# A row softmax on one core: sixteen partitions of the third tile loaded first, and no row of the second tile split

## The chip, the cores and the metric

The kernel runs on one core of one Trainium2 chip. The metric is the device time of a run in microseconds. The profile is one execution taken by the hardware profiler; its span runs from the first to the last instruction and is shorter than the time of a run by what lies around the program.

## The reference

```python
batch, seq, dim = 16, 1024, 512          # x: float32
x_scaled = x / 2.0
x_max = np.max(x_scaled, axis=-1, keepdims=True)
exp_x = np.exp(x_scaled - x_max)
return exp_x / np.sum(exp_x, axis=-1, keepdims=True)
```

There are 16384 rows of 512 numbers, 33.55 MB in and 33.55 MB out.

## The kernel before

Each of the 128 partitions works on 128 rows. They are cut into ten tiles along `TILES`, pairs of (rows per partition, place in the arena): 3, 5, and then eight times 15 rows. A tile is contiguous in memory, and partition p holds its rows p·r to p·r + r - 1, so a partition of a tile is one run of r·2048 bytes: 6 KB in tile 0, 10 KB in tile 1, 30 KB in the tiles from 2 on ("the third tile"). The arena in SBUF holds 98 rows per partition. Tiles 0 to 7 fill it; tiles 8 and 9 (`LATE`) reuse the places of tiles 0 to 3 and are loaded by GpSimd once those tiles' stores have landed.

The fast path leaves the maximum out. ACT takes the exponential of half of each row in place, with the row's sum as an accumulated output (`stats`); DVE takes the reciprocal of the sums and multiplies a group of rows in place; SyncE stores a tile when its multiplications are done. At the end a count of the sums that lie in a safe range is made through TensorE, and a slow path with the maximum (`rounds`) runs if a sum lies outside; in the profile it does not run.

What sets the order around the change:

- `early()` is put ahead of the start barrier of the program. There SyncE issues the load of tile 0, and ACT issues the load of tile 1.
- `loads()` comes behind the barrier: ACT issues the loads of tiles 2 to 7, one after another. Then ACT loads its table (line 200) and begins the exponentials.
- SyncE's DMAs go to one queue (q1 in the profile, which also carries all the stores), ACT's to another (q10), GpSimd's to a third (q0). All three share 16 DMA engines.
- TensorE waits for the tiles in order (line 194): a tile's semaphore `ld[t]` counts 16 for each DMA. For each tile it raises `s_go` by the number of chunks that begin there, and ACT takes these tokens one by one (`take`, line 140). A chunk is 3 rows for tile 0 and 5 rows after it.
- DVE waits for the exponentials of one to three chunks (line 166), multiplies (line 169), and SyncE stores (line 137).

The load of tile 1 is made of three DMAs: four rows of every partition, the last row of partitions 0 to 125, and the last row of partitions 126 and 127 (`SPREAD`, lines 113 to 121). So this tile's semaphore counts to 48.

Of the kernel before, what the change touches and what calls it, by code (L numbers as in the profile page):

```python
# [16 lines left out]
HEAD = [3]  # L17
E = 5

SPREAD = 1  # L20

TURN = 83

# [5 lines left out]
def kernel(  # L29
# [5 lines left out]
    nc = tc.nc  # L35
# [6 lines left out]
    xf = x.flatten_outer_dims()  # L42
    of = out.flatten_outer_dims()
    N, D = xf.shape
    P = nc.NUM_PARTITIONS
# [14 lines left out]
    tiles, base = [], 0  # L60
# [5 lines left out]
    def dram(ap, t):  # L66
        b, r, _ = tiles[t]
        return ap[b * P : (b + r) * P].rearrange("(p r) d -> p r d", r=r)

    def sb(t):  # L70
        _, r, at = tiles[t]
        return arena[:, at : at + r, :]
# [5 lines left out]
    owner = [max(t for t, (b, _, _) in enumerate(tiles) if b <= s) for s in starts]  # L78
# [12 lines left out]
    ld = [nc.alloc_semaphore(f"ld{t}") for t in range(len(tiles))]  # L91
# [4 lines left out]
    s_go = nc.alloc_semaphore("s_go")  # L96
# [13 lines left out]
    g_rec = nc.alloc_semaphore("g_rec")  # L110
    g_mul = nc.alloc_semaphore("g_mul")

    def load(eng, t):
        r = tiles[t][1]
        parts = [(0, P, 0, r)]
        if t == SPREAD:
            parts = [(0, P, 0, r - 1), (0, 126, r - 1, r), (126, P, r - 1, r)]
        for p, q, lo, hi in parts:
            eng.dma_start(  # L119
                out=sb(t)[p:q, lo:hi], in_=dram(xf, t)[p:q, lo:hi]  # L120
            ).then_inc(ld[t], 16)

    stored_by = {u: s_home[t] for t, us in LATE.items() for u in us}
    for t, (_, r, at) in enumerate(tiles):
# [26 lines left out]
            eng.reg_add(i, i, 1)  # L151

    def early():
        load(nc.sync, 0)
        load(nc.scalar, 1)

    def loads():
        for t in range(2, min(LATE)):
            load(nc.scalar, t)

    def program():

        for j, ks in enumerate(pairs):
# [3 lines left out]
                out=recip[:, b : b + c], in_=stats[:, b : b + c]  # L167
            )._wait_ge(s_exp, ks[-1] + 1).then_inc(s_rec, 1)
            nc.vector.tensor_mul(  # L169
                out=arena[:, a : a + c],  # L170
# [6 lines left out]
        for t, us in LATE.items():  # L177
# [3 lines left out]
            out=inside[:, :], in0=stats[:, :], scalar1=LO, scalar2=HI,  # L181
# [3 lines left out]
            out=inside[:, :], in0=inside[:, :], scalar=1.0, in1=stats[:, :],  # L185
# [3 lines left out]
            out=flag[:, :], in0=total[:, :], scalar1=float(N), scalar2=None, op0=Alu.is_ge,  # L189
# [1 line left out]


        for t in range(len(tiles)):
            nc.tensor.wait_ge(ld[t], 48 if t == SPREAD else 16).then_inc(s_go, owner.count(t))
        nc.tensor.wait_ge(s_ones, 1)
        nc.tensor.matmul(  # L196
            total[:, :], lhsT=count[:, :], rhs=ones[:, :], start=True, stop=True
# [3 lines left out]
        for k, c in enumerate(HEAD):  # L201
            take(nc.scalar, s_go, 1)
            for b in range(starts[k], starts[k] + c):
                ins = nc.scalar.activation(  # L204
                    out=arena[:, b], in_=arena[:, b], func=Exp, scale=0.5,
# [75 lines left out]
    entry.instructions = []  # L281
    nc.switch_bb("main", None)
    early()
    first = list(entry.instructions)
    at = next(k for k, i in enumerate(head) if type(i).__name__ == "InstDrain")
    entry.instructions = head[:at] + first + head[at:]
    act = []
    entry.instructions = list(entry.instructions) + [i for i in jumps if i not in act]
    nc.switch_body(here, parent=None, valid_engines=[i.engine for i in jumps])
    loads()  # L290
    program()


# [28 lines left out]
```

## Time and profile before

| | |
|---|---|
| time of a run, median of 3 | 159.94 us (159.79 to 166.79) |
| span of the profiled execution | 158.7 us |
| bytes moved | 67.11 MB, on average 423 GB/s over the span |
| packets | 3024, of these 336 under 512 B (the semaphore packets) and 720 under 8 KB |
| ACT busy | 80.8 us (51%) |
| DVE busy | 73.2 us (46%) |
| load of tile 0, issue to landing | 5.6 us |

The profiled execution has no time of its own beside its span; the median of the runs is 1.2 us above it. All numbers are microseconds unless marked otherwise. L119 is line 119 of the kernel; an engine name with a q behind it (SPq, ACTq) is the engine's instruction queue. The trace also holds a record of every DMA packet: its queue, start, duration and bytes, but not the number of its engine.

### The profile page before, as it was taken

The page shows a single profiled execution, that of the slowest core. Times are in us where ns is not written, and L with a number is a line of the kernel's source. Part 1 is how long each engine was busy: PE and PEld are TensorE (multiplying, and loading weights), DVE is VectorE, ACT ScalarE, POOL GpSimd, SP SyncE. Part 2 cuts the span into 40 slices and gives each one's busy share as a digit, 9 for nine tenths or more (in the row PEclk, how much of TensorE's full clock was granted, in tenths as well). Part 3 has the DMA queues.
Part 4 walks back from the last instruction along what each step waited for, and adds up shares of the span by engine and source line. Part 5 has one row for each costly group of instructions (what it writes and reads, how often), then busy time and mean ns, then how long its engine had stood idle before and what let it go on. Part 6 is the DMA issues. An engine that isn't in the chain of part 4 may idle for free. (4 is left out here: it accounts for less than half of the span.)

```text
span 158.7 us, 657 instructions
## 1 busy us (share of the span) xinstructions
PE 0.2 (0%) x2; PEld 0.1 (0%) x2; DVE 73.2 (46%) x27; ACT 80.8 (51%) x257; POOL 2.2 (1%) x8
## 2 busy tenths in 40 slices
PE   0000000000000000000000000000000000000000
PEld 0000000000000000000000000000000000000000
DVE  0047001992981990059500991008932981992000
ACT  0590598697498008940399001991597009940000
POOL 0000000000000000000000300000000000010000
DMA  7999998989999999999999999999999999999995
GB/s 271 382 496 396 463 437 324 480 382 485 410 457 410 457 410 449 418 449 418 441 426 441 426 434 434 426 441 426 441 418 449 418 449 410 457 403 465 403 457 256
DMA packets 3024, 67.11 MB, mean 423 GB/s; under 512 B 336, under 2 KB 336, under 8 KB 720
## 3 DMA queue, kind: packets, MB, share of 16 engines
q1 hardware_dynamic: 1584, 34.34, 50.4%
q10 hardware_dynamic: 1152, 24.90, 37.1%
q0 software_dynamic: 288, 7.86, 11.5%
HBM read 33.55 MB, written 33.55 MB: 423 GB/s over the span
## 5 line engine op out<-in xcount | busy, mean ns | idle before, releaser
L271 ACT ACTIVATE arena<-arena x125 | 76.8, 615 | 54.1 <-ACTq L140 54.1
L169 DVE TENSOR_TENSOR arena<-arena,recip 128x7680 f32<-128x7680 f32 (+2 forms) x12 | 70.2, 5847 | 0.4
L166 DVE RECIPROCAL recip<-stats 128x15 f32<-128x15 f32 (+2 forms) x12 | 2.7, 224 | 70.4 <-ACT arena L271 61.4
L271 ACT ACTIVATION_READ_ACCUMULATOR arena<-arena x125 | 23.4, 187 | 0.0
L200 ACT ACT_TABLE_LOAD x1 | 1.3, 1283 | 5.7 <-issue 5.7
L119 POOL DMA_DIRECT2D arena<-in_x_dram x2 | 1.3, 638 | 84.9 <-ACT arena L271 84.9
L204 ACT ACTIVATE arena<-arena 128x512 f32<-128x512 f32 x3 | 1.9, 619 | 0.0
L180 POOL TENSOR_SCALAR inside<-stats 128x128 f32<-128x128 f32 x1 | 0.6, 630 | 51.7 <-ACT arena L271 51.7
L204 ACT ACTIVATION_READ_ACCUMULATOR arena<-arena 128x1 f32 x3 | 0.6, 188 | 0.0
L196 PE MATMUL total<-ones,count 128*1 128x1 f32 x2 | 0.2, 164 | 143.9 <-DVE inside L184 143.9
L184 DVE SCALAR_TENSOR_TENSOR inside<-inside,stats 128x128 f32<-128x128 f32 x1 | 0.3, 282 | 0.0
L188 DVE TENSOR_SCALAR flag<-total 1x1 int32<-1x1 f32 x1 | 0.1, 146 | 0.3 <-PE total L196 0.3
L196 PEld LDWEIGHTS total<-ones,count 128*1 128x1 f32 x2 | 0.1, 80 | 143.9 <-DVE inside L184 143.9
L175 POOL MEMSET ones<- 128x1 f32 x1 | 0.1, 98 | 2.2 <-POOLq L37 2.2
L306 POOL MEMSET const-bfloat16-1.0<- 128x1 bf16 x1 | 0.1, 108 | 0.0
L306 POOL MEMSET const-uint8-127<- 128x1 uint8 x1 | 0.1, 108 | 0.0
L306 POOL MEMSET const-float32-0.0<- 128x1 f32 x1 | 0.1, 104 | 0.2 <-issue 0.2
L306 POOL MEMSET const-float32-1.0<- 128x1 f32 x1 | 0.1, 104 | 0.0
L184 DVE DVE_READ_ACCUMULATOR inside<-inside,stats 128x1 f32 x1 | 0.1, 80 | 0.0
## 6 DMA issues: line engine op xcount, KB each, us to landing
out_dram<-arena SPq DMA_DIRECT2D x8, 3840.0 KB, 26.2
arena<-in_x_dram ACTq DMA_DIRECT2D x6, 3840.0 KB, 46.7
arena<-in_x_dram POOLq DMA_DIRECT2D x2, 3840.0 KB, 33.6
out_dram<-arena SPq DMA_DIRECT2D x1, 1280.0 KB, 22.9
arena<-in_x_dram ACTq DMA_DIRECT2D x1, 1024.0 KB
arena<-in_x_dram SPq DMA_DIRECT2D x1, 768.0 KB, 5.6
out_dram<-arena SPq DMA_DIRECT2D x1, 768.0 KB, 14.6
arena<-in_x_dram ACTq DMA_DIRECT2D x1, 252.0 KB
```

Of the source, the lines that this page charges most:

```text
L119: eng.dma_start(out=sb(t)[p:q, lo:hi], in_=dram(xf, t)[p:q, lo:hi]).then_inc(ld[t], 16)
L166: nc.vector.reciprocal(out=recip[:, b : b + c], in_=stats[:, b : b + c])._wait_ge(s_exp, ks[-1] + 1).then_inc(s_rec, 1)
L169: nc.vector.tensor_mul(out=arena[:, a : a + c], in0=arena[:, a : a + c], in1=recip[:, b : b + c].unsqueeze(2).to_broadcast([P, c, D]),)._w ...
L175: nc.gpsimd.memset(ones[:, :], 1.0).then_inc(s_ones, 1)
L180: nc.gpsimd.tensor_scalar(out=inside[:, :], in0=stats[:, :], scalar1=LO, scalar2=HI, op0=Alu.max, op1=Alu.min,)._wait_ge(s_exp, len(sizes) ...
L184: nc.vector.scalar_tensor_tensor(out=inside[:, :], in0=inside[:, :], scalar=1.0, in1=stats[:, :], op0=Alu.mult, op1=Alu.is_equal, accum_ou ...
L188: nc.vector.tensor_scalar(out=flag[:, :], in0=total[:, :], scalar1=float(N), scalar2=None, op0=Alu.is_ge,)._wait_ge(s_tot, 1).then_inc(s_f ...
L196: nc.tensor.matmul(total[:, :], lhsT=count[:, :], rhs=ones[:, :], start=True, stop=True)._wait_ge(s_cnt, 2).then_inc(s_tot, 1)
L200: nc.scalar.preload_act_table(Exp)
L204: ins = nc.scalar.activation(out=arena[:, b], in_=arena[:, b], func=Exp, scale=0.5, accum_out=stats[:, b : b + 1],)
L271: ins = nc.scalar.activation(out=data, in_=data, func=Exp, scale=0.5, accum_out=stats[:, r : n_rows - E + 1 + r][:, bass.ds(now, 1)],)
L306: nc = _bacc.Bacc("TRN2", target_bir_lowering=False, num_devices=1)
```

## The change

SyncE's first DMA becomes the load of partitions 0 to 15 of tile 2: 16 packets of 30 KB, one on each DMA engine. The load of tile 0 comes right behind it on the same queue. ACT loads tile 1 whole in one DMA (128 packets of 10 KB), and behind the barrier it loads partitions 16 to 127 of tile 2 and then tiles 3 to 7 as before. The semaphore of tile 2 counts to 32, that of tile 1 to 16.

```diff
-SPREAD = 1
+PRIMER = 2
+FEW = 16
...
-    def load(eng, t):
-        r = tiles[t][1]
-        parts = [(0, P, 0, r)]
-        if t == SPREAD:
-            parts = [(0, P, 0, r - 1), (0, 126, r - 1, r), (126, P, r - 1, r)]
-        for p, q, lo, hi in parts:
-            eng.dma_start(
-                out=sb(t)[p:q, lo:hi], in_=dram(xf, t)[p:q, lo:hi]
-            ).then_inc(ld[t], 16)
+    def load(eng, t, part=slice(0, P)):
+        eng.dma_start(out=sb(t)[part], in_=dram(xf, t)[part]).then_inc(ld[t], 16)
...
     def early():
+        load(nc.sync, PRIMER, slice(0, FEW))
         load(nc.sync, 0)
         load(nc.scalar, 1)
 
     def loads():
         for t in range(2, min(LATE)):
-            load(nc.scalar, t)
+            load(nc.scalar, t, slice(FEW, P) if t == PRIMER else slice(0, P))
...
-            nc.tensor.wait_ge(ld[t], 48 if t == SPREAD else 16).then_inc(s_go, owner.count(t))
+            nc.tensor.wait_ge(ld[t], 32 if t == PRIMER else 16).then_inc(s_go, owner.count(t))
```

## The prediction

> **What bounds the kernel now.** I read the page's slices of the DMA engines first, then the waits, then the windows of the first microseconds, and last the records of single DMA packets.
>
> ```profile
> span 158.7 us, 657 instructions
> ...
> DMA  7999998989999999999999999999999999999995
> GB/s 271 382 496 396 463 437 324 480 382 485 410 457 410 457 410 449 418 449 418 441 426 441 426 434 434 426 441 426 441 418 449 418 449 410 457 403 465 403 457 256
> ...
> q1 hardware_dynamic: 1584, 34.34, 50.4%
> q10 hardware_dynamic: 1152, 24.90, 37.1%
> q0 software_dynamic: 288, 7.86, 11.5%
> HBM read 33.55 MB, written 33.55 MB: 423 GB/s over the span
> ```
>
> Each digit of the DMA row is the busy share of 16 engines in one fortieth of the span. Only the first and the last slice fall below 8; the three queues' shares add up to 99%. The kernel moves 67.11 MB and the engines never stop between. The computing engines wait for data instead:
>
> ```profile
> engine line waited for: us in total, times, longest us
> ...
> ACT arena L271 <- ACTq L140: 54.1, 8, 11.1
> ...
> DVE recip L166 <- ACT arena L271: 61.4, 9, 12.0
> ```
>
> ACT spends 54.1 us at line 140, where it takes the token that TensorE passes on when a tile has landed. So the end is set by bytes over rate, plus what is lost before the engines are full and after the first of them runs dry. The windows show both ends (columns: window, its length, busy time of PE, PEld, DVE, ACT and POOL, clock, DMA share, GB/s; a packet counts where it starts):
>
> ```profile
> 0.00:1.00 1.00, 0.00 (x0) 0.00 (x0) 0.00 (x0) 0.00 (x0) 0.21 (x4) 1.00 0.00 0
> 1.00:1.50 0.50, 0.00 (x0) 0.00 (x0) 0.00 (x0) 0.00 (x0) 0.00 (x0) 1.00 0.94 221
> 1.50:2.00 0.50, 0.00 (x0) 0.00 (x0) 0.00 (x0) 0.00 (x0) 0.00 (x0) 1.00 0.90 344
> 2.00:2.50 0.50, 0.00 (x0) 0.00 (x0) 0.00 (x0) 0.00 (x0) 0.00 (x0) 1.00 1.05 418
> ...
> 40.00:150.00 110.00, 0.19 (x2) 0.09 (x2) 58.49 (x20) 55.84 (x180) 1.90 (x3) 1.00 1.00 433
> ```
>
> Steady rate: 433 GB/s. 67.11 MB over 433 is 155.0 us. The first packet starts at 1.00 and the last ends at 158.18, so 2.2 us are lost between. Packet records place them: about 0.5 us up to 2.5 (two engines stand idle, and first packets of 6 KB take 0.24 to 0.75 us where later ones take 0.234), 0.2 us over the 2, 6 and 8 KB packets up to 6.5, 0.36 us while the first 30 KB packets of the third tile take 1.42 to 1.61 us each where the steady one takes 1.138, another 0.37 us between 25 and 30, and 0.5 us at the end; the rest is thin.
>
> The last loss is the spread between engines. Steady packets follow each other with the next start 4 ns before the last end, so I can follow 16 chains back from the end: they end from 157.38 to 158.18, on average at 157.7, and from their first 30 KB packet on (ended at 7.95 to 8.37, mean 8.08) each runs 149.3 to 150.2 us without a hole. What a chain gains or loses in the first 8 us it still has at the end.
>
> **What the change removes.** Two packet records matter. First, 14 engines start at 1.00 to 1.26, two only at about 2.1 and 2.4. Second, the last row of the second tile now goes as 126 and 2 partitions, 128 packets of 2 KB. Exactly two chains carry none of these: they end their last 8 KB packet at 6.44 and 6.47, the other fourteen at 5.7 to 6.1. I take these to be the late pair. The two partial transfers thus spare the pair 8 packets, which start every 80 ns: 0.64 us; each other engine takes 9 or 10. [...]
>
> After the change the second tile is 128 packets of 10 KB, 8 on every engine. A 10 KB packet takes 0.385 us in the stores of the same tile: 8 x 0.381 = 3.05 us. Before, 8 x 0.305 plus 9 x 0.080 = 3.16 us. So 14 engines save 0.1 us and the late pair pays 0.6. ACT also issues two DMAs fewer before its first barrier; the rows are below (start, duration, engine or its queue, line, what, count):
>
> ```profile
> 0.00 0.38 SPq L119 DMA_DIRECT2D arena<-in_x_dram  x1
> 0.13 5.51 ACTq L119 DMA_DIRECT2D arena<-in_x_dram  x9
> ...
> 5.67 1.28 ACT L200 ACT_TABLE_LOAD   x1 [5.67 <-issue]
> 6.96 0.63 ACT L204 ACTIVATE arena<-arena 128x512 f32<-128x512 f32 x1
> ```
>
> The partial rows took 0.67 and 0.24 us of issue; ACT passed the barrier at 1.93 and began its six loads at 2.66. Without them it starts these about 0.9 us sooner. This pays nothing: engines were not empty at 2.66, and will not be at 1.8.
>
> **What it adds and moves.** SP issues one more DMA first, 0.24 to 0.38 us of issue by the rows of the same line, and tile 0's issue moves behind it to about 0.4. The 16 packets of 30 KB start where the first 6 KB packets start now, 1.00 to 1.26. Their duration there is not in the trace: bounds 1.138 (steady) and 1.61 (slowest first one at 6.5); I take 1.5, the row of a first packet after none of its kind. The engines are then busy to about 2.65. The descriptors behind them: the ACT queue's first packet came 1.4 us after SP's, at 2.40, though issued 0.13 us after it; I read that as 128 descriptors taking 1.4 us to make. With 16 ahead of them, the next tile is ready well before 2.65, so the big packet covers the gap. Cover gone (a packet of 1.138 and a gap of 1.4), it costs 0.26 us.
>
> Sum for an on-time engine up to the end of equal work: 1.15 + 1.5 + 8 x 0.230 (tile 0) + 3.05 + 0.1 (slow first small packets) = 7.64; now 8.08. If the first 30 KB packet of the ACT queue is slow again, 0.36 comes back: 8.0. So 0.1 to 0.44 us gained on the mean; I take 0.25, between, as the slowness is seen once at a change from small to large packets and not explained. For the pair: lateness of 1.1 us at the start had shrunk to about 0.5 by 6.1. Unrelieved, it puts two chains 0.5 to 1.1 us behind, where now the last is 0.46 behind the mean; the low end if the others stall as they do now. If the pair starts on time, nothing. I take 0.7: last chain 157.72 - 0.25 + 0.7 = 158.17, against 158.18. Span 158.7, and with the 1.2 us by which the median of the runs shown (159.94) exceeds the span, **159.9 us**: no change.
>
> **Work off that path.** Tile 0 now queues behind the big packet and shares the engines packet by packet with tile 1, so its landing moves from 5.6 to about 7.5 or 8.3. That passes the table load, which ended at 6.95, by 0.5 to 1.3 us: queued behind are ACT's 8 rows of tiles 0 and 1, then DVE's first multiplications and the first two stores. ACT ended those rows at 11.98 and idled 5.73 us until 17.71 for the third tile, so this goes into that wait. The first store, now issued at 10.94, comes later by as much; engines carry loads meanwhile (tiles up to the eighth are queued by 5.6). The third tile's end moves with the total of bytes, not with the order. TensorE waits for 32 instead of 16 there: no instruction more. POOL's late loads start at 87.7 and see none of it.
>
> [...]
>
> **The rivals.**
> - *All chains start together* (chance 0.25). 16 descriptors are made in an eighth of the time; if the pair is late because its descriptors come last, it starts by 1.3. For it: the pair's start falls where the first DMA's descriptors end. Against it: the 14 others start 20 ns apart, not 90. Then 157.72 - 0.3 + 0.3 (spread) = 157.7, time 159.4.
> - *The pair carries all its lateness* (0.22), the slower case. The two engines are late for a reason that a DMA's size does not change; they start the big packet at 2.1 and 2.4 and, with no row spared, end 1.1 behind the mean: 157.72 - 0.15 + 1.1 = 158.67, time 160.4. It decides from a lateness of 0.7 on. For it: the pair is late now by 1.1. Against it: the others lost half of that lead by 6 us.
> - *The early tiles arrive too late* (0.04). If tiles 0 and 1 landed after 14.6 (17.71 less the 3.1 us of ACT's five rows), ACT would fall behind and stores would thin out the mix at the end. ACT is busy 51% in all, so it must be many us before the end moves: 163 or more. Rows speak against it.
> - *The change does nothing to the start*, because the ACT queue's tile is served first (0.04): 159.9 as well.
>
> Forecast itself: 0.45, 159.6 to 160.2. Range 159.2 to 160.8, both bounds of the pair and of the first packets taken in. A change is told from none at about 2%, 3.2 us here; all losses together are 2.2 us after the first packet and 1.0 before, so faster by that is nearly excluded (0.01), slower needs the early tiles' case (0.04), within it 0.95.
>
> **What would show it.** Right: 16 packets of 30 KB from 1.0, GB/s over 380 in the window 1.5 to 2.0, first exponential at 7.5 to 8.4, ACT's wait for the third tile shorter by as much, last DMA end within 0.3 of 158.2. The pair: two chains starting at over 2. Wrong: a slice of the DMA row below 9 after the third, a wait of ACT moved to the end, or an end spread under 0.5 or over 1.2 us.

## The result and the profile after

The changed kernel takes 168.36 us (median of 6 runs, 168.15 to 168.47) against 159.96 us before: a ratio of 1.0528, 95% interval 1.0515 to 1.0541. It is slower by 8.4 us; the forecast was no change, with 160.8 as the upper end. One run in several takes some 7 us longer (of these six before, two: 166.79 and 167.65), and all ratios here leave such runs out. The span of the profiled run grew from 158.7 to 166.8 us. From the page after, the lines that answer to those of before:

```profile
span 166.8 us, 656 instructions
...
DMA  9899989998999999999899899899899899899995
GB/s 130 300 379 268 250 236 432 455 436 383 440 464 442 390 464 442 390 464 449 383 464 457 376 464 464 368 464 464 376 457 457 383 457 457 383 457 457 405 435 250
...
q1 hardware_dynamic: 1616, 34.83, 50.2%
q10 hardware_dynamic: 992, 24.41, 37.9%
...
HBM read 33.55 MB, written 33.55 MB: 402 GB/s over the span
```

The busy row still shows 8 and 9 everywhere but in the last slice. The row under it tells the story: the first six slices of 4.2 us (up to 25 us) move 130, 300, 379, 268, 250 and 236 GB/s; from the seventh on it is as before. The engines are occupied and slow. The windows place it (window, length, busy time of PE, PEld, DVE, ACT, POOL, clock, DMA share, GB/s; a packet counts where it starts, hence the 860):

```profile
1.00:1.50 0.50, 0.00 (x0) 0.00 (x0) 0.00 (x0) 0.00 (x0) 0.00 (x0) 1.00 5.80 860
1.50:2.00 0.50, 0.00 (x0) 0.00 (x0) 0.00 (x0) 0.00 (x0) 0.09 (x1) 1.00 0.82 123
2.00:2.50 0.50, 0.00 (x0) 0.00 (x0) 0.00 (x0) 0.00 (x0) 0.01 (x1) 1.00 0.00 0
6.00:9.00 3.00, 0.00 (x0) 0.00 (x0) 0.00 (x0) 0.00 (x0) 0.00 (x0) 1.00 1.01 423
9.50:25.00 15.50, 0.00 (x0) 0.00 (x0) 2.06 (x3) 5.01 (x16) 0.00 (x0) 1.00 1.03 277
40.00:150.00 110.00, 0.19 (x2) 0.09 (x2) 63.82 (x22) 61.66 (x200) 1.90 (x3) 1.00 1.01 434
```

There are two slow stages. In the first, all 16 engines begin a 30 KB packet at 1.02 to 1.52, and no packet starts between 2.0 and 2.5: by the packet records these packets take 2.95 to 3.87 us (steady: 1.138), and the load's last semaphore packet comes at 6.0. From 6 to 9 tiles 0 and 1 run at 423 GB/s. Then the other 112 partitions of tile 2 come from 9.6 to 25, with packets of mostly 1.4 to 2.1 us; up to 17.3 the last packets of tile 0 take turns with them. After that the steady rate is the one of before, 434.

The waits and the timeline show who waited for it:

```profile
ACT arena L266 <- ACTq L134: 44.8, 8, 11.1
...
ACT arena L199 <- ACTq L134: 13.8, 1, 13.8
```

```profile
0.00 0.85 SPq L115 DMA_DIRECT2D arena<-in_x_dram  x2
0.12 4.55 ACTq L115 DMA_DIRECT2D arena<-in_x_dram  x7
...
4.70 1.28 ACT L195 ACT_TABLE_LOAD   x1 [4.70 <-issue]
19.83 0.63 ACT L199 ACTIVATE arena<-arena 128x512 f32<-128x512 f32 x1 [13.85 <-ACTq L134]
```

ACT now has a first wait of 13.8 us for tile 0, which landed 19.2 us after its issue. That looks like the loss, and is not: the DMA engines had loads to run throughout, and ACT catches up (its other waits shrink from 54.1 to 44.8). The second experiment, in which tile 0 lands 5.9 us after its issue and the run takes 168.63 us, bears this out. The loss is in the rate.

To sum it, I take from the packet records the lost time: the time minus the bytes moved by then over 432 GB/s, where a packet under way counts by its elapsed share. At 9 us it was 2.13 before and is 4.43 now; at 30 us 2.60 and 10.42; at 150 us 2.38 and 10.21. So all is lost by 30 us: 2.3 in the primer and 5.5 while the 112 partitions load, 7.8 of the 8.1 us by which the span grew.

### The profile page after: what moved, and what is told of

It is laid out like the page before. It is cut to its first block, busy times and chain, and to the rows that moved or that the text cites. A ratio compares the mean times of both kernels' runs of the same rounds, so it can differ in the third digit from the quotient of the medians.

```text
span 166.8 us, 656 instructions
## 1 busy us (share of the span) xinstructions
PE 0.2 (0%) x2; PEld 0.1 (0%) x2; DVE 73.2 (44%) x27; ACT 80.6 (48%) x257; POOL 2.2 (1%) x8
## 3 DMA queue, kind: packets, MB, share of 16 engines
q0 software_dynamic: 288, 7.86, 10.9%
## 5 line engine op out<-in xcount | busy, mean ns | idle before, releaser
L266 ACT ACTIVATE arena<-arena x125 | 76.6, 614 | 44.8 <-ACTq L134 44.8
L199 ACT ACTIVATE arena<-arena 128x512 f32<-128x512 f32 x3 | 1.9, 618 | 13.8 <-ACTq L134 13.8
## 6 DMA issues: line engine op xcount, KB each, us to landing
arena<-in_x_dram SPq DMA_DIRECT2D x1, 768.0 KB, 19.2
```

Of the source, the lines that this page charges most:

```text
L199: ins = nc.scalar.activation(out=arena[:, b], in_=arena[:, b], func=Exp, scale=0.5, accum_out=stats[:, b : b + 1],)
L266: ins = nc.scalar.activation(out=data, in_=data, func=Exp, scale=0.5, accum_out=stats[:, r : n_rows - E + 1 + r][:, bass.ds(now, 1)],)
```

## The experiments

Theories: **destination** (few partitions can take in only a part of what 16 engines deliver), **source** (the engines read neighbouring runs of memory, and this is slow), and **place** (the first packets of a run are slow whatever they are). In the destination theory a group is a set of partitions supposed to take in together no more than one engine delivers (27 GB/s, the steady 433 over 16).

**No primer.** Tile 1 stays whole, and tile 2 is one load again.

```diff
-        load(nc.sync, PRIMER, slice(0, FEW))
...
-            load(nc.scalar, t, slice(FEW, P) if t == PRIMER else slice(0, P))
+            load(nc.scalar, t)
```

> Tile 1 stays whole and tile 2 goes back to one load of 128 partitions by ACT; only the split of tile 1's last row is missing against before. Both theories (few partitions as destination; neighbouring runs of memory as source) expect no slow stage at 1 to 6 us nor at 9 to 25 us, and so nearly all of the 8.4 us back. What is left is the price of not splitting the row, which the prediction put at 0.64 us for the late pair of engines: 160.3 us, between 160.0 and 160.7.

Measured: 160.62 us, the median of the five runs that the ratio takes; ratio to before 1.0044 (1.0031 to 1.0058). The slow stages are gone:

```profile
span 159.5 us, 655 instructions
...
GB/s 275 482 393 381 450 444 358 472 406 457 393 470 393 447 416 424 431 431 439 424 454 408 454 408 408 454 416 447 424 447 416 439 431 431 431 439 431 431 431 239
```

So 7.7 of the 8.4 us belong to the split by partitions and its order, and 0.7 to giving up the split of tile 1's last row. The size was expected (0.64), its cause only in part. A chain is the sequence of packets on one DMA engine, as the prediction follows them. Two chains begin their first 30 KB packet at 6.99 and 7.00 where the others begin at 6.27 to 6.79, which I take to be the late pair; but at the end eight chains are about 1.3 us behind the other eight, and most of these lost it in slow packets between 47 and 100 us. That later loss stays unexplained.

**The same split, later.** ACT issues both parts behind the barrier; SyncE begins with tile 0.

```diff
     def early():
-        load(nc.sync, PRIMER, slice(0, FEW))
...
+            if t == PRIMER:
+                load(nc.scalar, t, slice(0, FEW))
             load(nc.scalar, t, slice(FEW, P) if t == PRIMER else slice(0, P))
```

> Tile 2 is split into partitions 0 to 15 and 16 to 127 as in the change, but ACT issues both behind the barrier and SyncE begins with tile 0. If the split by partitions is what costs, wherever it stands: 167.5 to 168.8 us, with packets of 30 KB of 2 to 4 us and of 1.6 to 2.1 us as in the changed kernel, now after tile 1. If it is the place at the very start (engines not yet running): 160.0 to 161 us, with packets of 1.14 us.

Measured: 168.63 us, ratio 1.0553 (1.0534 to 1.0572). The place theory falls: the slow stage has moved to the third slice, behind tiles 0 and 1.

```profile
span 167.4 us, 656 instructions
...
GB/s 277 342 117 235 285 285 430 426 426 448 426 419 455 426 433 448 411 448 433 419 426 441 433 426 433 411 441 441 411 441 448 411 433 455 419 426 448 433 419 257
```

**Source or destination.** On the kernel without primer, SyncE loads 480 KB more ahead of tile 0, into tile 7's place, 16 runs of 30 KB each. The bytes alone are worth 1.14 us (0.49 MB over the steady 433 GB/s).

```diff
     def early():
+        nc.sync.dma_start(
+            out=sb(7)[0:16], in_=dram(xf, 2)[0:16]
+        ).then_inc(s_probe, 16)
         load(nc.sync, 0)
...
+            if t == 7:
+                nc.scalar.wait_ge(s_probe, 16)
             load(nc.scalar, t)
```

The four runs differ in these slices alone: out `[0:16]` and in `[0:16]`; out `[0:16]` and in `[0:128:8]`; out `[0:32:2]` and in `[0:16]`; out `[0:128:8]` and in `[0:16]`.

> On the kernel without primer and without split, SyncE first loads 16 runs of 30 KB once more, into the place of tile 7, which is loaded over it later; the data of this load is not used. Here source and destination are those of the primer: neighbouring runs of tile 2 to partitions 0 to 15. Both theories: landing at 5.5 to 6.0 us as in the changed kernel, packet records of 3 to 3.9 us; about 4.5 us for it.

> The same extra load, but its 16 runs lie 240 KB apart in memory (every eighth run of tile 2); still to partitions 0 to 15. Destination theory: as in the run before, landing at 5.5 to 6.0 us, packets of 3 to 3.9 us. Source theory: packets of 1.14 to 1.6 us, landing at 2.5 to 3.3 us.

> The same extra load, neighbouring runs of memory, but to partitions 0, 2, 4 ... 30. Source theory: as with partitions 0 to 15, 5.5 to 6.0 us. [...]

> The same extra load, neighbouring runs of memory, but to partitions 0, 8, 16 ... 120. Source theory: 5.5 to 6.0 us again. [...] Destination theory with groups of eight neighbours: 16 groups, packets of 1.14 to 1.6 us, landing at 2.5 to 3.2 us.

The row of the extra load among the DMA issues of each run, in this order (KB, us from issue to landing); the table has a single run's time and the packet records:

```profile
arena<-in_x_dram SPq DMA_DIRECT2D x1, 480.0 KB, 6.6
```

```profile
arena<-in_x_dram SPq DMA_DIRECT2D x1, 480.0 KB, 7.2
```

```profile
arena<-in_x_dram SPq DMA_DIRECT2D x1, 480.0 KB, 7.9
```

```profile
arena<-in_x_dram SPq DMA_DIRECT2D x1, 480.0 KB, 7.6
```

| source | destination | packets start | packet, us | run, us |
|---|---|---|---|---|
| neighbours | 0 to 15 | 1.02 to 1.42 | 2.53 to 3.88 | 163.11 |
| 240 KB apart | 0 to 15 | 1.02 to 2.07 | 2.60 to 4.04 | 163.37 |
| neighbours | 0, 2 ... 30 | 3.68 to 4.22 | 1.62 to 2.27 | 162.56 |
| neighbours | 0, 8 ... 120 | 3.60 to 4.26 | 1.57 to 2.24 | 161.88 |

The source does not matter here: runs 240 KB apart are no faster (2.60 to 4.04 against 2.53 to 3.88). The destination does: spread out, no packet takes more than 2.27, twice the steady 1.138, as 8 groups for 16 engines would give. (The spread packets run behind the first packets of tile 1, but so do the 16 neighbours in the run that splits later, and those take 3.04 to 4.36.) Groups of eight neighbours would be 4 for 0, 2 ... 30 and 16 for 0, 8 ... 120, but every second partition does about as well (1.62 to 2.27) as every eighth (1.57 to 2.24), so the groups are not eight neighbours. All four landing times were missed: the loads to 0 to 15 landed after 6.6 and 7.2 us, not 5.5 to 6.0, and the packets of the spread loads begin 2.6 us later, so these landed last of all (7.9 and 7.6) although they moved faster. Why such a load starts late I did not follow up.

**The size of it.** Tile 2, in its normal place, in halves and in eight loads of 16.

```diff
-FEW = 16
+FEW = 64
```

```diff
+            if t == PRIMER:
+                for j in range(8):
+                    load(nc.scalar, t, slice(FEW * j, FEW * j + FEW))
+            else:
+                load(nc.scalar, t)
```

The first diff stands on the kernel that splits later. The eight loads are run once more with `slice(j, P, 8)`.

> As the run before, but tile 2 is split into partitions 0 to 63 and 64 to 127. [...] By rows: if a half of the partitions takes half of the steady 433 GB/s, tile 2 takes 18.2 us in place of 9.1: 169.4 us, slower than the split into 16 and 112. Source theory: the engines read runs 120 KB apart, between the 30 KB of the slow first load (about 110 to 150 GB/s) and the 210 KB of the 112 partitions (about 280): 9 to 24 us for tile 2 as well; so this run tests the size only, and a time under 165 us speaks against the destination theory.

> No primer; tile 2 comes in eight loads of 16 neighbouring partitions, all issued by ACT in tile 2's place. [...] If only the first such load is slow, or if the number of loads costs and not their partitions: under 166 us.

> As the run before, with the same number of loads, packets and bytes, but each load takes every eighth partition. Destination theory with 8 groups for such a set: 217 GB/s, 18.1 us in place of 9.1: 169 to 171 us. If the number of loads costs: the same time as with neighbours.

Measured, a single run each: 168.14, 184.07 and 168.36 us. The window from 7 to 12, in which only tile 2 moves, for halves, 16 neighbours and every eighth:

```profile
7.00:12.00 5.00, 0.00 (x0) 0.00 (x0) 1.93 (x2) 4.99 (x17) 0.00 (x0) 1.00 0.99 203
```

```profile
7.00:12.00 5.00, 0.00 (x0) 0.00 (x0) 0.53 (x2) 3.82 (x10) 0.00 (x0) 1.00 0.96 111
```

```profile
7.00:12.00 5.00, 0.00 (x0) 0.00 (x0) 0.00 (x0) 2.74 (x6) 0.00 (x0) 1.00 0.99 203
```

Against the steady 433: about a half for 64 neighbours, about a half for every eighth, about a quarter for 16 neighbours. Divided by one engine's steady 27 GB/s, 203 is the rate of 7.5 engines and 111 that of 4.1, by my estimate; which partitions share a group is not shown. Eight loads of equal size differ by 15.7 us through their partitions, so the number of loads is not the price. (Their sources differ too, neighbours against runs 240 KB apart, but that made no difference above.) The halves and the eighths have lost 10.5 and 10.9 us by 30 us and nothing more by 150. The halves, expected to be slower than 16 and 112, came out level with them. The totals of the halves and the eighths lie 0.6 to 2.6 us under my sums (169.4, and 169 to 171), which did not count that stores of tile 0 run beside the slow packets: by the packet records the eight loads of neighbours move 116 GB/s from 10 to 26 us, and about 150 with the stores after it.

**A primer that reaches all partitions.** SyncE first loads rows 0 and 1 of tile 2 for every partition, 512 KB; then the same with the last row of tile 1 split again.

```diff
-FEW = 16
+FEW = 2
...
-    def load(eng, t, part=slice(0, P)):
-        eng.dma_start(out=sb(t)[part], in_=dram(xf, t)[part]).then_inc(ld[t], 16)
+    def load(eng, t, rows=None):
+        rows = rows or slice(0, tiles[t][1])
+        eng.dma_start(out=sb(t)[:, rows], in_=dram(xf, t)[:, rows]).then_inc(ld[t], 16)
...
-            load(nc.scalar, t, slice(FEW, P) if t == PRIMER else slice(0, P))
+            load(nc.scalar, t, slice(FEW, tiles[t][1]) if t == PRIMER else None)
```

> A primer that reaches all partitions: SyncE first loads rows 0 and 1 of tile 2 for all 128 partitions (512 KB, 8 packets of 4 KB per engine), then tile 0; ACT loads tile 1 whole and later the other 13 rows of tile 2. Destination theory: no slow stage; as without primer (160.75 us) within 0.5 us, more likely 0.1 to 0.3 slower for 128 packets more. If a load ahead of tile 0 costs as such: 163 us or more.

> As the run before, and the last row of tile 1 is split into 126 and 2 partitions again, as in the kernel before. The split was worth 0.44% without primer: 160.0 to 160.3 us; not under 159.7, because the losses that a primer could fill were 0.5 us in all.

Measured: 159.86 us, ratio to before 1.0000 (0.9991 to 1.0008); and with the split row 160.03 us, 1.0015 (1.0002 to 1.0028). A primer that reaches all partitions costs about 0.2 us at most by these ratios. The GB/s row of the first:

```profile
GB/s 234 460 412 432 473 416 416 432 416 383 460 442 427 427 442 427 442 427 442 427 442 427 442 419 450 411 458 388 481 388 481 388 481 388 481 372 481 388 473 272
```

This is the closest control of the change: the same two queues load tile 2 in two parts, but cut by rows, and there is no slow stage (2.2 us lost by 30 us, where the change lost 10.42). So it is the cut by partitions that costs, in the second part of the tile too. The first of the two runs even makes up for the unsplit row, which I had not expected: without primer that lost 0.44%. Its 16 chains end from 157.35 to 157.91, a spread of 0.56 where before it was 0.80 and without primer 1.80. It equals the kernel before; nothing here beats it.

## Why the prediction was wrong

- **What bounds the kernel** was right: bytes over rate, and what is lost early is lost at the end. The steady rate between 40 and 150 us was 428 to 435 GB/s in the seven kernels measured over it, and no computing engine set the end: in the changed kernel the last instruction of DVE ended at 147.7 us and the last packet at 166.4.
- **The step that failed** is the duration of the 16 packets: "bounds 1.138 (steady) and 1.61 (slowest first one at 6.5); I take 1.5". They took 2.95 to 3.87, and the window from 1.5 to 2.0, named as a sign with over 380 GB/s, moved 123. Both bounds came from loads that fill all 128 partitions, and I never asked where the 16 packets go. A load of 16 neighbours moved 111 to 119 GB/s in the eight-loads run; 0.49 MB over that is 4.1 to 4.4 us for the primer alone.
- **The step that is missing** is the price of the remaining 112 partitions, which I costed as nothing: 7 packets per engine at the full rate. This was the larger part, 5.5 of 7.8 us. Packets of 1.4 to 2.1 us would fit engines sharing groups there too, but this is not shown: how 112 partitions are dealt out to the engines the records do not tell. This part is measured and not derived, and why 112 partitions load slowly stays open.
- **One more transfer** had no term of its own in my sum, and none above about 0.2 us is seen: the two-row primer is one load more on SyncE's queue, and the ratios are 1.0000 and, with the split row, 1.0015. The rate was the point.
- **Tile 0's landing** was put at 7.5 to 8.3 and came at 19.2, so the first exponential began at 19.83 instead of 7.5 to 8.4. Tile 1's packets started first (3.97; tile 0's first at 7.3), and tile 0's last three packets per engine took turns with the slow 30 KB ones. As forecast, though, this went into ACT's waits: where the same split came later, tile 0 landed before ACT had its table, and the time was the same (168.63).
- **The rival of the early tiles** ("arrive too late", 0.04) has its condition met, as tile 0 landed after 14.6, and its time of 163 or more as well. Its mechanism is not the one: that same later split has the time without the late landing.
- **The late pair** started at 1.50 and 1.52 instead of about 2.1 and 2.4. That fits the rival that ties its lateness to the number of descriptors (1.4 us for 128 is my estimate from first packets at 1.00 and 2.40), but the load of 16 runs 240 KB apart has as few, and its last two packets start at 2.04 and 2.07. So the rival stays open, and it could not show in the time. My slower rival (160.4) named the pair and missed the cause.
- **The split row** was put at 0.64 us and was 0.7 without primer, about the size, with a later part that I can't explain; with the two-row primer it was worth nothing.

## What to carry to other kernels

Price a DMA by where its bytes go in SBUF as well as by how many engines carry it: 16 packets on 16 engines moved at about a quarter of the rate (111 of 433 GB/s) when they landed in 16 neighbouring partitions, and the load of the other 112 was slow too (277 GB/s from 9.5 to 25 us, with the last packets of tile 0 among it). Where a tile must be cut, cut it by rows and keep all 128 partitions in each piece; here that cost nothing measurable (159.86 us, ratio 1.0000). A busy row of nines says that engines are occupied (in the changed kernel nines stand over 130 GB/s and over 464); read the GB/s row under it before calling a stage full.

## What the runs showed of the hardware that was not expected

- Two loads of 64 neighbouring partitions, one behind the other, ran at 203 GB/s, not at 433: the partitions of the second half did not help the first.
- A load to every second or eighth partition began its packets at 3.6 to 4.3 us, 2.6 us after a load to neighbours issued at the same moment. ACT's tile 1, issued after it, ran first there, from 1.14 us.
- With 16 packets ahead, ACT's tile 1 (issued at 0.12) ran before SyncE's tile 0 (issued after the primer): first packets at 3.97 and 7.30.
